# A hybrid decoder trunk on one core: rotary swap by DMA, main products in runs of 12 and 24, and a rearranged gate stage

## The chip, the core and the metric

One Trainium2 chip, of which this kernel uses one core. The core has TensorE (PE, with its weight loads shown apart as PEld), VectorE (DVE), ScalarE (ACT), GpSimd (POOL) and SyncE (SP), which here does nothing but start DMA transfers. The metric is the device time of one execution in microseconds.

## The reference, cut to what matters

One layer of a decoder: x goes through RMSNorm, one input projection, three attention head groups ("patterns") with windows and dilations (128, 1), (512, 4) and (2048, 16), a Mamba-2 branch (SSD) whose output is gated by silu(z) and normed, one output projection, and then a SwiGLU feed-forward. A prompt of 1024 positions and 8 decode positions with caches of 2048 rows are computed together. The parts that the change touches:

```python
def rope(x, pos):                       # q and k of all three patterns
    x1, x2 = xf[..., :half], xf[..., half:]          # half = 32
    return jnp.concatenate([x1 * cos - x2 * sin, x2 * cos + x1 * sin], axis=-1)
...
p = jnp.exp(sc - m); den = jnp.sum(p, axis=-1, keepdims=True)
o = jnp.einsum('brnhqk,brnkhd->brnhqd', p, vb) / den       # 128 keys and the 128 before them
...
def ssd_gate_out(y, xs, z, d_skip, ssd_norm_w):
    y = (y + d_skip[:, None] * xs).reshape(..., SSD_INNER) * jax.nn.silu(z)
    return rmsnorm(y, ssd_norm_w)
...
attn = merge_patterns(outs, lses)                          # softmax of the three lse, 512 columns
mix = jnp.concatenate([attn, ssm], axis=-1) @ w_out
```

## The kernel before

Everything lies transposed: features on the 128 partitions, the T = 1032 positions (1024 of the prompt, then 8 of decode) along the free axis, in three chunks CH of 344 columns. A matrix product in fp32 is made of three products on rounded parts: weight high times activation high, weight low times activation high, weight high times activation low. `unit` makes one 128 x 344 result from 8 blocks of 128 inputs, so 24 products, all on L175; `gemm` loads one 128 x 1024 weight (`load_w`: a DMA, then ACT rounds it to `wh` on L163 and DVE subtracts to `wl` on L164) and runs `unit` for the three chunks, each with a copy out of PSUM by ACT. PSUM has eight banks; the products of `unit` have the two of pool `psg` (tag g), the small work has the others: `pss` (tag sp, two banks) and the rest.

The order of instructions on each engine is fixed when the kernel is built, by a scheduler that takes, of the instructions whose inputs are ready in its own model of time, the one with the lowest priority number. `prio(kind)` hands out these numbers from counters: "evac" 1 million (copies out of PSUM and what follows at once), "w" 5 million (weight loads), "side" 10 million (attention, SSD and all small work), "late" 20 million (merging of the attention outputs and cache values), "main" 50 million (products of `unit`). So PE fills with main products whatever side work leaves, and a piece of side work may stand between any two main products. `behind(ins, prev)` fixes that an instruction stands behind another on its own engine. `next_copy` keeps the copies out of PSUM in order.

In time: up to some 200 us the projections of conv inputs; 200 to 590 us pattern 0 with the SSD work; to 890 us patterns 1 and 2; 850 to 968 us the gate stage; 968 to 1000 us the first products of the gated values with w_out (L955); to 1200 us output projection and norms; 1216 to 1592 us the feed-forward's inputs, then its outputs and the end.

In a pattern, each of four pairs of heads (hp) takes one `do_v` and two `do_qk` (q, then k), each of which is a projection of three units. The rotation in `do_qk` wants a copy `sw` of the projection `rw` in which each two neighbouring groups of 32 partitions have changed places: four ACT copies of 32 x 1032 on L615. POOL multiplies `sw` by sin on L616, DVE multiplies `rw` by cos on L617, and DVE adds both into `qr`. There are 24 rotations. `attend` then takes 8 steps per pair of heads, 96 in all: PE scores `sps` (L646), DVE adds the mask and takes the maximum (L652), ACT takes two exponentials with their sums (L660), PE transposes `ptp` (L667), a copy `pt` out of PSUM (ACT L671 in one step of four, DVE L673 in the other three), PE values `nps` (L680).

The gate stage: for each of 8 tiles k, the projection z (three units, copied to `zt` by ACT on L903), silu on ACT (L910), times the SSD result `yg`, loaded from DRAM `y_d`, on DVE (L911), the square on ACT (L916), and the sum of squares over the tiles, `acc`, by POOL (L918). `zt` has two buffers. In between stands "late" work: the merge (`nt` times weights on POOL L855, two adds on DVE L856 and L857, the rounding `ah` on ACT L858, `al` on DVE L859), 16 blocks of it; and the decode positions' values: for each b of 8, three cache blocks `cvt` times probabilities, added on DVE (L878), and summed over partitions by a product with `sel` (L879). After the tiles ACT and DVE split the gated values into `sh` (L924) and `sl` (L925), 128 x 1032 each; products with `ones` (L931 on `acc`, L932 on the last `zt`) sum the squares over partitions for the norm `rt`; and the first 96 products with w_out (L955) take two output tiles m and two chunks c at once.

Of the kernel before, what the change touches and what calls it, by code (L numbers as in the profile page):

```python
# [36 lines left out]
HB = T // 4  # L37
RATE = (0.35, 0.43)
# [11 lines left out]
def trunk(tc, a, o):  # L50
    nc = tc.nc
    ctr = {"evac": 1_000_000, "w": 5_000_000, "side": 10_000_000, "late": 20_000_000, "main": 50_000_000}
# [113 lines left out]

    def unit(ps, w, hs, ls, c, ch=CH):
# [14 lines left out]
    def gps(name="g", cw=CW):  # L182
# [4 lines left out]
        return q.tile([P, 512], F32, tag="ap", name=name)[:, :cw]  # L187

    def gemm(src, cols, hs, ls, evac, cc=(0, 1, 2), share=False):
# [440 lines left out]
    def attend(g, hp, qr, kr, vt):  # L630
        nh = nhp.tile([P, S], F32, tag="nh", name="nh")
        for j in range(8):
# [126 lines left out]
    with prio("side"):  # L759
        dec_scores(0)  # L760
    pattern(1)
# [49 lines left out]
    cvp = pool(rst, "cvp", 5, side="right")  # L811
# [49 lines left out]

    with prio("late"):
# [4 lines left out]
        for b in range(NB):  # L867
# [11 lines left out]
            nc.tensor.matmul(ops[:NB], sel[:, b * NB:(b + 1) * NB], vts[0], start=(b == 0), stop=(b == NB - 1))  # L879
# [12 lines left out]


    with prio("side"):
        rt = rowp.tile([P, T], F32, tag="row", name="rt")
        acc = gp.tile([P, T], F32, tag="acc", name="acc", bufs=1)
    yg = []
    for k in range(KT):
        zt = gp.tile([P, T], F32, tag="zt", name="zt")

        def ev(c, ps, zt=zt):
            c0, c1 = CH[c]
            return nc.scalar.copy(zt[:, c0:c1], ps)  # L903

        gemm(a["w_in"][36 + k], 1024, xh, xl, ev)
        with prio("side"):
# [587 lines left out]
```

## Time and profile before

| | us |
|---|---|
| median of 3 runs | 1859.24 |
| lowest and highest | 1858.23, 1863.11 |
| profiled execution, its own time | 1865.26 |
| span of that execution's profile | 1863.5 |
| PE busy in it | 1776.0 |
| DVE, ACT, POOL busy | 1141.2, 781.4, 320.0 |
| mean granted clock of TensorE | 0.98 of full speed |

The span reaches from the first to the last recorded instruction; 1.8 us of the execution lie around it. Busy times count an instruction from its start to its end, so matmuls that overlap in PE's pipeline count as one busy stretch, and a busy PE may still be slow. What PE loses is better seen in how many products it starts in a stretch.

### The profile page before, as it was taken

To read this page: it belongs to the slowest core of one execution; us is meant where nothing else is said; L and a number is where in the kernel's file an instruction comes from. 1 tells how busy PE (TensorE), PEld (TensorE's weight loads), DVE (VectorE), ACT (ScalarE), POOL (GpSimd) and SP (SyncE) were. 2 spreads that over 40 slices of the span, in tenths; PEclk is the share of its full clock that TensorE was granted. 3 is DMA by queue.
4 is the path that set the end of the run, shared out by engine and by line. 5 is a ranking of instruction groups with operands and counts; after the bars stand their busy time and mean duration, and the time that the engine had idled before them with its cause. 6 is when DMAs were issued, how large, how long until landed. Compare 5 with 4: busy or idle time off the path is not lost.

```text
span 1863.5 us, 30669 instructions
## 1 busy us (share of the span) xinstructions
PE 1776.0 (95%) x12183; PEld 1659.1 (89%) x12183; DVE 1141.2 (61%) x2228; ACT 781.4 (42%) x1433; POOL 320.0 (17%) x218
## 2 busy tenths in 40 slices
PE   8999999999998999999878999999999999999995
PEld 6999877888887889988758999999999999999995
DVE  6545666766765454446667499886666666423338
ACT  5533554455554555556333235532222222431133
POOL 0000245444234221123442301000000000000020
PEclk9999999999999999999988999999999999999998
DMA  4322344434334243346566355355545445976686
GB/s 157 135 100 79 97 127 125 128 121 116 114 103 156 90 137 103 123 152 224 171 167 182 101 160 180 110 199 171 176 151 183 167 151 197 351 264 215 207 314 206
DMA packets 135198, 298.59 MB, mean 160 GB/s; under 512 B 18432, under 2 KB 85600, under 8 KB 133648
## 3 DMA queue, kind: packets, MB, share of 16 engines
q1 hardware_dynamic: 135056, 296.64, 48.4%
q8 instruction: 95, 1.56, 0.3%
q14 instruction: 47, 0.39, 0.1%
HBM read 247.49 MB, written 137.10 MB: 206 GB/s over the span
## 4 chain that ended last, share of the span: by engine, by line
PE 37%; DVE 8%; DMA 3%; issue 1%; ACT 1%; POOL 1%; DVEq 0%; SPq 0%; POOLq 0%; ACTq 0%
PE fb L1217 20%; PE g L175 16%; DMA nt<-n_d 1%; PE g L955 1%; DVE xr L1043 1%; POOL nt L855 1%; DVE fl L1058 1%; DVE nacc L1000 1%; DVE mix L1055 0%; DVE nt L856 0%; DVE fac L1341 0%; DMA wr<-in_w_fin 0%; DVE nt L857 0%; DMA out_yT<-fac 0%; DMA wt<-w_d 0%
## 5 line engine op out<-in xcount | busy, mean ns | idle before, releaser
L175 PE MATMUL g<-xh,wh 128*128 128x344 f32 x1344 | 443.6, 330 | 9.3 <-ACT zt L903 5.1
L175 PE MATMUL g<-xl,wh 128*128 128x344 f32 x1344 | 440.3, 328 | 1.5 <-DVE xl L231 1.5
L175 PE MATMUL g<-xh,wl 128*128 128x344 f32 x1344 | 439.2, 327 | 0.5 <-DVE wl L164 0.5
L175 PEld LDWEIGHTS g<-xh,wh 128*128 128x128 f32 x1344 | 255.6, 190 | 19.0 <-ACT zt L903 5.6
L175 PEld LDWEIGHTS g<-xh,wl 128*128 128x128 f32 x1344 | 256.2, 191 | 12.3 <-issue 11.0
L175 PEld LDWEIGHTS g<-xl,wh 128*128 128x128 f32 x1344 | 256.1, 191 | 10.6 <-issue 7.7
L1217 PE MATMUL fb<-fh,wsl 128*128 128x258 f32 x1216 | 222.5, 283 | 0.1
L1217 PEld LDWEIGHTS fb<-fh,wsl 128*128 128x128 f32 x1216 | 188.0, 189 | 0.4 <-DVE fs L1113 0.3
L1217 PE MATMUL fb<-fl,wsl 128*128 128x258 f32 x608 | 171.9, 283 | 0.0
L164 DVE TENSOR_TENSOR wl<-wr,wh 128x1024 fp32r<-128x1024 f32 (+1 forms) x93 | 111.7, 1202 | 80.2 <-ACT wh L163 79.9
L175 PE MATMUL g<-hh,wh 128*128 128x344 f32 x432 | 138.1, 320 | 0.1
L175 PE MATMUL g<-hh,wl 128*128 128x344 f32 x432 | 137.8, 319 | 0.0
L175 PE MATMUL g<-hl,wh 128*128 128x344 f32 x432 | 136.9, 320 | 0.0
L163 ACT CAST wh<-wr 128x1024 fp32r<-128x1024 f32 (+1 forms) x93 | 92.5, 995 | 95.0 <-PE g L175 91.5
L660 ACT ACTIVATE sm<-sm,ngm 128x128 f32<-128x128 f32 (+1 forms) x192 | 84.9, 443 | 106.1 <-DVE ngm L656 102.2
L1300 POOL TENSOR_TENSOR ow<-wr,ow 128x512 fp32r<-128x512 f32 x8 | 10.9, 1395 | 658.8 <-ACT ow L1299 658.8
L616 POOL TENSOR_TENSOR sw<-sw,sin 128x1032 f32<-128x1032 f32 x24 | 72.8, 3032 | 251.0 <-ACT sw L615 187.6
L1217 PEld LDWEIGHTS fb<-fl,wsl 128*128 128x128 f32 x608 | 114.9, 189 | 0.0
L615 ACT COPY sw<-rw 32x1032 f32<-32x1032 f32 x96 | 101.0, 1052 | 1.4
L586 ACT COPY rw<-g 128x344 f32<-128x344 f32 x108 | 47.2, 443 | 111.8 <-PE g L175 71.5
L1221 DVE TENSOR_TENSOR fo<-fp,fb 128x258 f32<-128x258 f32 x152 | 62.8, 420 | 45.4 <-PE fb L1217 43.3
L175 PEld LDWEIGHTS g<-hh,wh 128*128 128x128 f32 x432 | 81.2, 188 | 0.3 <-ACT fac L1284 0.3
(362 smaller groups left out, 3801.2 us busy)
## 6 DMA issues: line engine op xcount, KB each, us to landing
out_skv<-in_cache SPq DMA_DIRECT2D x64, 1023.5 KB, 5.7
wr<-in_w_in SPq DMA_DIRECT2D x56, 512.0 KB, 3.7
out_skv<-in_cache SPq DMA_DIRECT2D x16, 1022.0 KB, 5.6
wr<-in_w_out SPq DMA_DIRECT2D x24, 512.0 KB, 3.7
hr<-hid_d SPq DMA_DIRECT2D x22, 516.0 KB, 6.2
hid_d<-fo SPq DMA_DIRECT2D x38, 258.0 KB, 4.5
wg<-in_w_fin SPq DMA_DIRECT2D x19, 512.0 KB, 4.2
wu<-in_w_fin SPq DMA_DIRECT2D x19, 512.0 KB, 5.1
```

Of the source, the lines that this page charges most:

```text
L163: nc.scalar.copy(wh[:, :cols], wr[:, :cols])
L164: nc.vector.tensor_tensor(out=wl[:, :cols], in0=wr[:, :cols], in1=wh[:, :cols], op=ALU.subtract)
L175: last = nc.tensor.matmul(ps, x[:, ws], y[:, c0:c1], start=(k == 0 and j == 0), stop=(k == n - 1 and j == 2))
L586: return nc.scalar.copy(rw[:, c0:c1], ps)
L615: nc.scalar.copy(sw[q * 32:(q + 1) * 32, 0:T], rw[s * 32:(s + 1) * 32, :])
L616: nc.gpsimd.tensor_tensor(out=sw[:, 0:T], in0=sw[:, 0:T], in1=sin, op=ALU.mult)
L660: nc.scalar.activation(out=sm[:, h, :nk], in_=sm[:, h, :nk], func=AF.Exp, scale=SCALE, bias=ngm[:, g, j, i:i + 1], accum_out=den[:, g, j, ...
L855: nc.gpsimd.tensor_tensor(out=nt, in0=nt, in1=wt, op=ALU.mult)
L955: nc.tensor.matmul(pq[m][c], ws[m][j == 1][:, k * P:(k + 1) * P], (sl if j == 2 else sh)[k][:, CH[c][0]:CH[c][1]], start=(k == 0 and j == ...
L1000: nc.vector.tensor_tensor(out=acc, in0=acc, in1=sq, op=ALU.add)
L1217: nc.tensor.matmul(ps, x[:, ks], y, start=(k == 0 and j == 0), stop=(k == 3 and j == 2))
L1221: return nc.vector.tensor_tensor(out=dst, in0=x, in1=y, op=ALU.add)
```

## The change

1. Runs. Of a unit's products, only each 12th carries the priority "main", the others a new priority "run" (3 million, ahead of weights and side work); from pattern 1 on, only each 24th. So side work on PE can stand only between runs of 12, later of 24, products.
2. Rotary swap. The four ACT copies of each rotation become four DMA transfers of 32 x 1032 fp32 (132 KB), started by SP. The product with sin moves from POOL to DVE.
3. All `pt` copies are on ACT: 72 more of them.
4. Gate stage. The loop over z stands ahead of the cache values in the code. From tile 4 on, the z units alternate over the two pools `psg` and `pss`, four banks. Each `sel` product stands behind the last product of a named z unit (table CACHE: tile, chunk). The cache values' pool has 6 buffers, not 5.
5. Sum of squares. POOL adds only the tiles up to 5; the products with `ones` take the squares of tiles 6 and 7 directly from their `zt` (nine products, not six), and stand behind the 48th of the 96 first products with w_out (`middle`).
6. The split into `sh` and `sl` is made in two column parts, 0 to 688 for all eight tiles, then 688 to 1032.

```diff
--- before
+++ after
@@ top of the file and trunk @@
+CACHE = ((4, 0), (4, 1), (4, 2), (5, 0), (5, 2), (6, 1), (7, 0), (7, 2))
...
-    ctr = {"evac": 1_000_000, "w": 5_000_000, "side": 10_000_000, "late": 20_000_000, "main": 50_000_000}
+    ctr = {"evac": 1_000_000, "run": 3_000_000, "w": 5_000_000, "side": 10_000_000, "late": 20_000_000, "main": 50_000_000}
@@ unit, gps, gemm @@
+    run = [12]
...
-        with prio("main"):
-            for k in range(n):
-                ws = slice(k * P, (k + 1) * P)
-                for j, (x, y) in enumerate(((wh, hs[k]), (wl, hs[k]), (wh, ls[k]))):
+        for k in range(n):
+            ws = slice(k * P, (k + 1) * P)
+            for j, (x, y) in enumerate(((wh, hs[k]), (wl, hs[k]), (wh, ls[k]))):
+                with prio("main" if (3 * k + j) % run[0] == 0 else "run"):
                     last = nc.tensor.matmul(ps, x[:, ws], y[:, c0:c1], start=(k == 0 and j == 0),
                                             stop=(k == n - 1 and j == 2))
...
-        return q.tile([P, 512], F32, tag="ap", name=name)[:, :cw]
+        return q.tile([P, 512], F32, tag="sp" if q is pss else "ap", name=name)[:, :cw]
...
+            if ends:
+                ends[0][ends[1], c] = last
@@ do_qk @@
-                nc.scalar.copy(sw[q * 32:(q + 1) * 32, 0:T], rw[s * 32:(s + 1) * 32, :])
-            nc.gpsimd.tensor_tensor(out=sw[:, 0:T], in0=sw[:, 0:T], in1=sin, op=ALU.mult)
+                nc.sync.dma_start(out=sw[q * 32:(q + 1) * 32, 0:T], in_=rw[s * 32:(s + 1) * 32, :])
+            nc.vector.tensor_tensor(out=sw[:, 0:T], in0=sw[:, 0:T], in1=sin, op=ALU.mult)
@@ attend @@
-            if j % 2 and j % 4 < 2:
-                nc.scalar.copy(dst, tp[:, :2 * nk])
-            else:
-                nc.vector.tensor_copy(dst, tp[:, :2 * nk])
+            nc.scalar.copy(dst, tp[:, :2 * nk])
@@ between dec_scores(0) and pattern(1) @@
+    run[0] = 24
@@ gate stage: the z loop now stands ahead of the cache values @@
-    cvp = pool(rst, "cvp", 5, side="right")
+    cvp = pool(rst, "cvp", 6, side="right")
...
+    zlast, zts = {}, []
     for k in range(KT):
+        if k == 4:
+            gpools[:] = [psg, pss]
         zt = gp.tile([P, T], F32, tag="zt", name="zt")
...
+        zts.append(zt)
+        gemm(a["w_in"][36 + k], 1024, xh, xl, ev, ends=(zlast, k))
...
-                if k < KT - 1:
+                if k < KT - 2:
                     nc.gpsimd.tensor_tensor(out=acc, in0=acc, in1=zt, op=ALU.add)
...
-            nc.tensor.matmul(ops[:NB], sel[:, b * NB:(b + 1) * NB], vts[0], start=(b == 0), stop=(b == NB - 1))
+            behind(nc.tensor.matmul(ops[:NB], sel[:, b * NB:(b + 1) * NB], vts[0], start=(b == 0), stop=(b == NB - 1)),
+                   zlast[CACHE[b]])
...
+    gpools[:] = [psg]
     sh, sl = [], []
     with prio("evac"):
         for k in range(KT):
-            hi = actp.tile([P, T], F32R, tag="act", name=f"sh{k}")
-            lo = actp.tile([P, T], F32R, tag="act", name=f"sl{k}")
-            nc.scalar.activation(out=hi, in_=yg[k], func=AF.Copy, scale=nw(SSD_NORM, k))
...
+            sh.append(actp.tile([P, T], F32R, tag="act", name=f"sh{k}"))
+            sl.append(actp.tile([P, T], F32R, tag="act", name=f"sl{k}"))
+        for cs_ in (slice(0, 2 * CW), slice(2 * CW, T)):
+            for k in range(KT):
+                hi, lo = sh[k][:, cs_], sl[k][:, cs_]
+                nc.scalar.activation(out=hi, in_=yg[k][:, cs_], func=AF.Copy, scale=nw(SSD_NORM, k))
+                nc.vector.scalar_tensor_tensor(out=lo, in0=yg[k][:, cs_], scalar=nw(SSD_NORM, k), in1=hi,
+                                               op0=ALU.mult, op1=ALU.subtract)
-        for c, (c0, c1) in enumerate(CH):
-            sp_ = att_ps("ptp")
-            nc.tensor.matmul(sp_[:, :CW], ones, acc[:, c0:c1], start=True, stop=False)
-            nc.tensor.matmul(sp_[:, :CW], ones, zt[:, c0:c1], start=False, stop=True)
-            rms(sp_[:, :CW], rt[:, c0:c1])
...
+                        if (k, m, j, c) == (3, 1, 2, 1):
+                            middle = ins
+    with prio("evac"):
+        for c, (c0, c1) in enumerate(CH):
+            sp_ = att_ps("ptp")
+            behind(nc.tensor.matmul(sp_[:, :CW], ones, acc[:, c0:c1], start=True, stop=False), middle)
+            for i in (KT - 2, KT - 1):
+                nc.tensor.matmul(sp_[:, :CW], ones, zts[i][:, c0:c1], start=False, stop=(i == KT - 1))
+            rms(sp_[:, :CW], rt[:, c0:c1])
```

SP, at a rotation of pattern 0 (`hs`, `out_sssm`, `in_ssm`: decode states of the SSD; `wr`: a weight), before:

```order
L469 DMA out_sssm<-hs_2000 128x4x128
L463 DMA hs_2018<-in_ssm 128x4x128
L469 DMA out_sssm<-hs_2009 128x4x128
L463 DMA hs_2027<-in_ssm 128x4x128
L469 DMA out_sssm<-hs_2018 128x4x128
L488 DMA xg_2036<-xs_d_326 128x4x128
L469 DMA out_sssm<-hs_2027 128x4x128
L148 DMA wr_4372<-in_w_in 128x1024
```

After, at the same place:

```order
L475 DMA out_sssm<-hs_2000 128x4x128
L621 DMA sw_3908<-rw_3823 32x1032 x3
L469 DMA hs_2018<-in_ssm 128x4x128
L149 DMA wr_4372<-in_w_in 128x1024
L621 DMA sw_3908<-rw_3823 32x1032
L475 DMA out_sssm<-hs_2009 128x4x128
L469 DMA hs_2027<-in_ssm 128x4x128
L475 DMA out_sssm<-hs_2018 128x4x128
```

The transfers of the swap stand in the one queue of SP; three are together, and the load of a state and of a weight come ahead of the fourth. In 14 of the 24 rotations the four are parted so.

PE, near the end of pattern 2 (`g`: a main unit; `nps`: values of the last attention step of a pair of heads; `vtp`: transposes of v for the next, by `do_v`), before:

```order
L175 MATMUL g_8809<-xl2_122,wh_8752 128x344
L175 MATMUL g_8809<-xh3_115,wh_8752 128x344
L175 MATMUL g_8809<-xh3_115,wl_8753 128x344
L175 MATMUL g_8809<-xl3_123,wh_8752 128x344
L680 MATMUL nps_7815<-pt_7859,vt_7523 64x128 x2
L604 MATMUL vtp_7956<-ident_90,vp_7954 128x128 x4
L175 MATMUL g_8809<-xh4_116,wh_8752 128x344
L175 MATMUL g_8809<-xh4_116,wl_8753 128x344
```

After, where the same `nps_7815` and `vtp_7956` stand:

```order
L652 MATMUL sps_8162<-qr_8157,qr_8061 128x128 x2
L683 MATMUL nps_7815<-pt_7827,vt_7523 64x128 x2
L652 MATMUL sps_8163<-qr_8157,qr_8061 128x128 x2
L673 MATMUL ptp_7843<-ident_90,sm_7837 128x128 x2
L683 MATMUL nps_7815<-pt_7846,vt_7523 64x128 x2
L673 MATMUL ptp_7856<-ident_90,sm_7850 128x128 x2
L652 MATMUL sps_8195<-qr_8157,qr_8061 128x128 x2
L652 MATMUL sps_8196<-qr_8157,qr_8061 128x128 x2
L683 MATMUL nps_7815<-pt_7859,vt_7523 64x128 x2
L610 MATMUL vtp_7956<-ident_90,vp_7954 128x128 x4
L791 MATMUL pnp_8387<-ident_90,pn0_8388 128x32
L791 MATMUL pnp_8387<-ident_90,pn1_8391 128x32
```

What stood between main products in pieces of two to six is now one piece with several attention steps and no main product in it. There are two such long pieces without main products: four steps near the 137th unit of PE, and eight steps near the 152nd. The piece begins where the first z tile's `zt` is to be used a second time: that wants its `yg` read, and the load of `yg` from `y_d` stands behind the last `vtp` of pattern 2 by the memory that it takes over. Before, that `vtp` stood five units ahead of this place.

PE, at the end of the z tiles (`g_9445` and `g_9330`: the last z unit; `ptp_9508`: sum of squares; `g_9547` to `g_9548` and `g_9543` to `g_9544`: first products with w_out), before:

```order
L175 MATMUL g_9445<-xh6_118,wh_9388 128x344
L175 MATMUL g_9445<-xh6_118,wl_9389 128x344
L175 MATMUL g_9445<-xl6_126,wh_9388 128x344
L175 MATMUL g_9445<-xh7_119,wh_9388 128x344
L931 MATMUL ptp_9508<-acc_8749,ones_91 128x344
L175 MATMUL g_9445<-xh7_119,wl_9389 128x344
L175 MATMUL g_9445<-xl7_127,wh_9388 128x344
L955 MATMUL g_9547<-sh0_9476,wh_9536 128x344
L955 MATMUL g_9548<-sh0_9476,wh_9536 128x344
L955 MATMUL g_9547<-sh0_9476,wl_9537 128x344
```

After:

```order
L179 MATMUL g_9330<-xh7_119,wl_9274 128x344
L179 MATMUL g_9330<-xl7_127,wh_9273 128x344
L913 MATMUL nps_9364<-cvt_9449,sel_9361 8x512
L958 MATMUL g_9543<-sh0_9475,wh_9532 128x344
L958 MATMUL g_9544<-sh0_9475,wh_9532 128x344
L958 MATMUL g_9543<-sh0_9475,wl_9533 128x344
L958 MATMUL g_9544<-sh0_9475,wl_9533 128x344
L958 MATMUL g_9543<-sl0_9476,wh_9532 128x344
```

The product with `acc` is gone from among the last z products, and stands after 48 products with w_out. The last `sel` product has come to the end of the last z unit. `sel` products stood before at the units 158.2 (three), 159.3, 160, 160.9, 163 and 164.2, counted in units of 24 main products; after, at 160 (two), 161 (three), 164, 166 and 168.

## Rows read from the trace of the kernel before

**Rows 1.** Part 1 of the page: busy us (share of the span) xinstructions.

```profile
PE 1776.0 (95%) x12183; PEld 1659.1 (89%) x12183; DVE 1141.2 (61%) x2228; ACT 781.4 (42%) x1433; POOL 320.0 (17%) x218
```

**Rows 2.** Stretches: length, busy us (xinstructions) of engines, granted clock, DMA share, GB/s.

```profile
50.00:100.00 50.00, 49.99 (x318) 49.99 (x319) 29.84 (x42) 24.19 (x32) 0.50 (x5) 1.00 0.34 117
...
900.00:950.00 50.00, 37.68 (x188) 28.60 (x186) 34.42 (x44) 13.01 (x22) 24.54 (x16) 0.94 0.69 188
950.00:1000.00 50.00, 41.54 (x206) 36.52 (x206) 37.22 (x45) 24.86 (x35) 19.18 (x9) 0.82 0.52 141
```

**Rows 3.** PE groups by line and form: xcount | busy us, mean ns | idle before.

```profile
L175 PE MATMUL g<-xh,wh 128*128 128x344 f32 x1344 | 443.6, 330 | 9.3 <-ACT zt L903 5.1 <-ACT rw L586 3.5 <-ACT wh L163 0.7
...
L646 PE MATMUL sps<-qr 64*128 64x128 f32 x208 | 25.8, 316 | 11.6 <-DVE qr L620 11.6
...
L497 PE MATMUL xt<-ident,xg 128*128 128x128 f32 x64 | 10.1, 280 | 7.7 <-DMA xg<-xs_d 7.7
...
L879 PE MATMUL nps<-cvt,sel 128*8 128x512 f32 x16 | 9.6, 705 | 7.6 <-DVE cvt L878 6.0 <-issue 1.6
...
L931 PE MATMUL ptp<-acc,ones 128*128 128x344 f32 x6 | 2.8, 562 | 3.0 <-POOL acc L918 3.0
```

**Rows 4.** ACT in order of time, at 947 us: start, us, instruction [idle before].

```profile
946.85 0.41 ACT L858 CAST ah<-nt 128x256 fp32r<-128x256 f32 x1 [6.25 <-DVE nt L857]
947.16 0.44 ACT L903 COPY zt<-g 128x344 f32<-128x344 f32 x1
```

**Rows 5.** PE in order of time, first products with w_out, 975 to 985 us.

```profile
975.60 0.94 PE L955 MATMUL g<-sh,wh 128*128 128x344 f32 x2 [2.19 <-ACT sh L924]
...
977.67 0.78 PE L955 MATMUL g<-sh,wh 128*128 128x344 f32 x2
...
982.16 0.94 PE L955 MATMUL g<-sl,wh 128*128 128x344 f32 x2 [1.43 <-DVE sl L925]
...
985.20 0.54 PE L955 MATMUL g<-sh,wh 128*128 128x344 f32 x2
```

**Rows 6.** Groups of the rotation and of the exponentials, by line and form.

```profile
L615 ACT COPY sw<-rw 32x1032 f32<-32x1032 f32 x96 | 101.0, 1052 | 1.4
...
L616 POOL TENSOR_TENSOR sw<-sw,sin 128x1032 f32<-128x1032 f32 x24 | 72.8, 3032 | 251.0 <-ACT sw L615 187.6 <-PE ptp L667 25.4 <-PE g L175 24.7
...
L617 DVE TENSOR_TENSOR rw<-rw,cos 128x1032 f32<-128x1032 f32 x24 | 38.6, 1610 | 18.6 <-ACT sw L615 18.6
...
L660 ACT ACTIVATE sm<-sm,ngm 128x128 f32<-128x128 f32 x104 | 41.0, 395 | 57.8 <-DVE ngm L656 54.3 <-PE nps L680 2.7 <-DVE stt L701 0.5
...
L660 ACT ACTIVATION_READ_ACCUMULATOR sm<-sm,ngm 128x1 f32 x192 | 36.0, 187 | 0.0
```

**Rows 7.** ACT and POOL in order of time, one rotation, 584 to 600 us.

```profile
584.52 4.24 ACT L615 COPY sw<-rw 32x1032 f32<-32x1032 f32 x4
...
596.79 2.36 POOL L616 TENSOR_TENSOR sw<-sw,sin 128x1032 f32<-128x1032 f32 x1
```

**Rows 8.** DMA issues (KB each, median us to landing), and SP's time for one.

```profile
yg<-y_d SPq DMA_DIRECT2D x8, 516.0 KB, 8.3
...
bg<-bc_d SPq DMA_DIRECT2D x16, 128.0 KB, 3.4
...
out_pv<-rw SPq DMA_DIRECT2D x4, 64.0 KB, 1.5
...
L627 SPq DMA_DIRECT2D out_pk<-qr x8: 338/344/352, 225.2 to 844.1; - x8
```

**Rows 9.** PE and ACT in order of time, one attention step, 765 to 767 us.

```profile
765.68 0.32 PE L175 MATMUL g<-xl,wh 128*128 128x344 f32 x1
765.93 0.44 PE L680 MATMUL nps<-pt,vt 128*64 128x128 f32 x4
...
766.49 0.41 PE L175 MATMUL g<-xh,wh 128*128 128x344 f32 x1
...
766.77 0.37 ACT L671 COPY pt<-ptp 128x256 f32<-128x256 f32 x1 [1.70 <-PE ptp L667]
```

More of the change, by code (lines that the diff above doesn't have):

```diff
@@ L859, in trunk, with ev @@
                 nc.vector.tensor_tensor(out=al[:, hp, qs], in0=nt[:, 0], in1=ah[:, hp, qs], op=ALU.subtract)
+    with prio("side"):
+        rt = rowp.tile([P, T], F32, tag="row", name="rt")
+        acc = gp.tile([P, T], F32, tag="acc", name="acc", bufs=1)
+    yg = []
+    zlast, zts = {}, []
+    for k in range(KT):
+        if k == 4:
+            gpools[:] = [psg, pss]
+        zt = gp.tile([P, T], F32, tag="zt", name="zt")
+        def ev(c, ps, zt=zt):
+            c0, c1 = CH[c]
+            return nc.scalar.copy(zt[:, c0:c1], ps)
+        zts.append(zt)
+        gemm(a["w_in"][36 + k], 1024, xh, xl, ev, ends=(zlast, k))
+        with prio("side"):
+            yt = mixp.tile([P, T], F32, tag="mix", name=f"yg{k}")
+            nc.sync.dma_start(out=yt, in_=y_d[k])
+        with prio("evac"):
+            nc.scalar.activation(out=zt, in_=zt, func=AF.Silu)
+            nc.vector.tensor_tensor(out=yt, in0=yt, in1=zt, op=ALU.mult)
+            yg.append(yt)
+            if k == 0:
+                nc.scalar.activation(out=acc, in_=yt, func=AF.Square)
+            else:
+                nc.scalar.activation(out=zt, in_=yt, func=AF.Square)
+                if k < KT - 2:
+                    nc.gpsimd.tensor_tensor(out=acc, in0=acc, in1=zt, op=ALU.add)
     with prio("late"):
@@ L891, in trunk @@
     rst.close()
[L894 to L906, printed above, removed]
-            yt = mixp.tile([P, T], F32, tag="mix", name=f"yg{k}")
-            nc.sync.dma_start(out=yt, in_=y_d[k])
-        with prio("evac"):
-            nc.scalar.activation(out=zt, in_=zt, func=AF.Silu)
-            nc.vector.tensor_tensor(out=yt, in0=yt, in1=zt, op=ALU.mult)
-            yg.append(yt)
-            if k == 0:
-                nc.scalar.activation(out=acc, in_=yt, func=AF.Square)
-            else:
-                nc.scalar.activation(out=zt, in_=yt, func=AF.Square)
-                if k < KT - 1:
-                    nc.gpsimd.tensor_tensor(out=acc, in0=acc, in1=zt, op=ALU.add)
+    gpools[:] = [psg]
     sh, sl = [], []
@@ L921, in trunk @@
         for k in range(KT):
[L922 to L934 removed]
+            sh.append(actp.tile([P, T], F32R, tag="act", name=f"sh{k}"))
+            sl.append(actp.tile([P, T], F32R, tag="act", name=f"sl{k}"))
+        for cs_ in (slice(0, 2 * CW), slice(2 * CW, T)):
+            for k in range(KT):
+                hi, lo = sh[k][:, cs_], sl[k][:, cs_]
+                nc.scalar.activation(out=hi, in_=yg[k][:, cs_], func=AF.Copy, scale=nw(SSD_NORM, k))
+                nc.vector.scalar_tensor_tensor(out=lo, in0=yg[k][:, cs_], scalar=nw(SSD_NORM, k), in1=hi,
+                                               op0=ALU.mult, op1=ALU.subtract)
     gpools.append(psa)
     ngp[0] = 0
[L939 removed]
     mix = [mixp.tile([P, T], F32, tag="mix", name=f"mix{m}") for m in range(KT)]
@@ L954, in trunk @@
                     for c in range(2):
-                        nc.tensor.matmul(pq[m][c], ws[m][j == 1][:, k * P:(k + 1) * P],
+                        ins = nc.tensor.matmul(pq[m][c], ws[m][j == 1][:, k * P:(k + 1) * P],
                                          (sl if j == 2 else sh)[k][:, CH[c][0]:CH[c][1]],
                                          start=(k == 0 and j == 0), stop=(k == KT - 1 and j == 2))
+                        if (k, m, j, c) == (3, 1, 2, 1):
+                            middle = ins
+    with prio("evac"):
+        for c, (c0, c1) in enumerate(CH):
[4 more added lines that the diff above has]
+            rms(sp_[:, :CW], rt[:, c0:c1])
+    gst.close()
+    np_ = pool(mst, "np", 2, side="left")
     with prio("evac"):
```

8 lines of the change are left out of this document (1 added, 7 removed).

## The prediction

> **What bounds the kernel now.** I read the busy shares first. PE is busy for 95% of the span and the next engine, DVE, for 61% [rows 1], so time is to be had only where PE starts fewer products than it could. The table of stretches shows where. At full clock with nothing in the way PE started 318 products in 50 us, 0.157 us each [rows 2]. In the gate stage, 900 to 1000 us, it started 188 + 206 = 394 matmuls of all kinds [rows 2]. At 0.157 these are 62 us. The 16 `sel` and 12 sum matmuls among them are longer; their spans of 0.705 and 0.562 us [rows 3] overlap, and I give them 7 us more. So 100 - 69 = 31 us are lost there, at a clock granted at 0.94 and 0.82 [rows 2]. Then I read the PE groups by the idle time before them, to see who is waited for: in the gate stage `zt` copies 5.1, `sel` 7.6, `acc` 3.0 us [rows 3], then `sh` 2.19 and `sl` 1.43 [rows 5]. Outside it, scores wait 11.6 us for `qr` and transposes 7.7 us for `xg` [rows 3]. Feed-forward and tail are untouched.
>
> **The gate stage, part by part.** *Sum of squares.* The products with `acc` stood among the last z products and made PE wait 3.0 us for POOL [rows 3]. They now stand behind 48 products of w_out, 7.5 us later at 0.157, and POOL has two adds less: **-3.0**. Three more products with `ones` come in, at most 0.562 us each [rows 3] and partly overlapped: **+1.0** (0.5 to 1.7).
>
> *Split in column parts.* PE waited 2.19 us for the first `sh` and 1.43 for an `sl` [rows 5]. Parts of 688 of 1032 columns are ready after two thirds of the time, and the third part follows while chunks 0 and 1 are multiplied. I take half: **-1.8** (0 to -3.6).
>
> *Clock.* From 975.60 to 985.20 us PE started 26 products of w_out [rows 5]. At 0.157 these are 4.1 us; they took 9.6, of which 1.43 were the wait for `sl`. The other 4.1 us is the slow clock after the waits ahead of them: the pace shown, 2.07 us for the six products from 975.60 to 977.67 [rows 5], is about half of full. With the waits ahead of it cut, PE should come there at full clock, except for some: **-3.3** (0 to -4.1).
>
> *Copies of z.* The group of first products waited 5.1 us for `zt` copies [rows 3]. ACT's timeline shows one cause: the copy at 947.16 stood behind a rounding `ah`, before which ACT had waited 6.25 us for the merge on DVE [rows 4]. ACT works in order, and that order is not changed. With four banks in place of two PE can run up to three units, 3 x 24 x 0.157 = 11 us, past a late copy, longer than the 6.25: **-4.6** (0 to -5.1). Against it stands that `zt` has only two buffers: a copy into a third tile still waits for the square of the first, so the banks help against a late copy and not against a late tile.
>
> *Cache values.* `sel` waited 7.6 us, 6.0 of it for DVE's adds [rows 3]. Pinned one to five units later (3.8 us each) with one buffer more, most should find their input ready. The last stands behind the last z unit and can still wait: **-5.6** (-2 to -7.6).
>
> Together -3.0 + 1.0 - 1.8 - 3.3 - 4.6 - 5.6 = **-17.3 us** of the 31 lost.
>
> **The rotary swap.** A rotation had four ACT copies of 1.05 us and a POOL product of 3.03 us on average [rows 6], and POOL was often not free: in the one at 584 us the copies ended at 588.8 and the POOL product began at 596.79 [rows 7], 8 us later. In its place come four transfers: SP needs 0.34 us for each issue [rows 8]. No row shows such a transfer of 132 KB. The nearest are 128 KB landing in 3.4 us and 64 KB in 1.5 [rows 8]; I take 2.4, between them. Then DVE's sin product, like its cos product 1.61 us [rows 6]. So 1.4 + 2.4 + 1.6 = 5.4 us (4.5 to 6.4) stand against 4.2 + 3.0 plus the queue on POOL, 7.2 to 15 us. Of the 11.6 us that scores waited for `qr` [rows 3] I take **-8** (-11.6 to 0). SP's queue is the risk, a rival below. DVE gains 24 x 1.61 = 39 us and loses 72 copies; ACT loses 101 us [rows 6] and gains 72 x 0.37 [rows 9] = 27. Both are further from PE's bound than before. The 7.7 us for `xg` [rows 3] is a wait of SSD work for loads in the same queue; with side work in larger pieces these have more time: **-3** (0 to -6, and +2 if the new transfers hold them up).
>
> **Runs of 12 and 24.** They change no product, only where side work may stand. Changes between main and side work on PE go from 216 to about 140. A change costs little: from the main product at 765.68 to the side product at 765.93 is 0.25 us, 0.09 over 0.157 [rows 9]. 76 of these are 7 us at most: **-2** (0 to -7). The cost is elsewhere. A pair's attention steps now come once in a unit or two, so attention falls behind, and at the end of pattern 2 there are 12 steps with no main product between them (four, then eight). A step alone goes at ACT's pace: two exponentials with their sums, 2 x (0.395 + 0.187) [rows 6], and a copy of 0.37 [rows 9], 1.53 us, where PE's own matmuls take about 1.1 (six of them took 765.93 to 766.49, 0.56 us [rows 9], and a step has some twelve). That is 12 x 0.45 = 5.4 us idle. After the eight, PE needs the `zt` that waits for the load of `yg`, 8.3 us [rows 8], and the product and copy behind it, about 1.8 us; against it some three steps' work, 4.6 us, and some decode work: about 5 us are left. Together **+10** (5 if the load comes early, 20 if nothing covers it and the clock falls in the gap).
>
> Patterns together: -8 - 3 - 2 + 10 = **-3**. In all -17.3 - 3 = -20.3. The profiled execution took 1865.26 us, 6 above the median; against it the sum gives 1845, and against the median of 1859.24, with which the new median will be compared, **1839 us**. A change of 0.3%, 5.6 us, is about what a measurement of this kernel can tell from none.
>
> A page of the Trainium skill speaks to the swap's price: "SBUF — State Buffer", section "Door 1: The DMA port swizzle (why `[64,N]` ≈ `[32,N]`)", says that DMA bandwidth goes by how many of 16 ports the partitions reach, and that 32 neighbouring partitions lie on half of them. By an estimate from that page's 435 GB/s, 132 KB would take 0.6 us in place of 0.3, later by 0.3 us for one. [...] No row here shows a transfer of this shape.
>
> **The rivals.** *A, all waits go.* The named waits of the gate stage go whole (3.0 + 3.6 + 4.1 + 5.1 + 7.6 - 1.0 = 22.4), the patterns give 11.6 + 6 + 2, and the bare stretches cost 5: -37, **1822**. For it: the clock falls only after waits, and one wait less saves the next. Against: the last cache value and the silu chain stay serial. Chance 0.17.
>
> *B, the bare stretches cost their upper end.* If the eight steps and the load of `yg` stand wholly bare, the runs cost 20 us, and the lower clock that follows a gap (0.82 in the last such stretch [rows 2]) takes some 4 more. -20.3 + 14 = -6, **1853 to 1858**, within 0.3% for the most part. For it: in the order no main product stands there. Against: the decode work in the same piece. Chance 0.13.
>
> *C, the transfers come late: slower.* The swap now goes through SP's single queue, where an instruction that waits holds all behind it. In 14 of 24 rotations the four transfers are parted by loads or stores that wait for other engines, and DVE's sin product, waiting, holds the masks of other steps and the `wl` of the next weight. PE then stands without scores and without weights. Each of the 24 rotations that costs 20/24 = 0.83 us more than forecast takes the gain away. At 1.5 us each it is +36 - 20 = +16: **1875**. For it: a load in this queue can take 8.3 us to land [rows 8], against the 2.4 taken. Against: main products cover most of a late `qr`, since each rotation has three units of 3.8 us beside it, and in 24 rotations before, with a chain of 7 to 15 us, PE waited only 11.6 us in all [rows 3]. Chance 0.18.
>
> *D, four banks that do nothing.* If tile buffers and not banks held the z units, the -4.6 goes and little else: 1844, inside the forecast.
>
> **How the numbers follow.** Forecast, with D, 1828 to 1850: 0.52. A 0.17, B 0.13, C 0.18. Faster by over 0.3% (below 1853.7): the forecast and A, 0.69. Within: most of B, 0.12. Slower: C and a tail of B, 0.19. For 8 in 10 the range takes in the forecast, most of A (all waits gone, and some of the clock with them: 1815) and B, and the milder half of C: 1815 to 1866.
>
> **What would show it.** In the stretches 900 to 1000 us of before, after: some 17 us less for the same products, and a clock near full from the z tiles into w_out. No wait for `acc` before the first products with w_out; `sel` waits below 2 us. The score's wait for `qr` below 4 us; swap transfers landing near 2.4 us, and DVE idle ahead of the sin product without PE idle beside it. Two idle stretches of PE at the end of pattern 2, 10 us together. Wrong would be: idle PE ahead of scores or ahead of main products for `wl`, transfers of over 5 us (C); over 20 us idle at the last steps (B); z products still waiting for `zt` (D).

## The result and the profile after

The changed kernel takes 1921.93 us (median of 4 runs, 1919.58 to 1924.64), where the kernel before took 1861.17 in the same session: 1.031 times as long, 95% interval 1.0282 to 1.0338. It was forecast at 1839 and 0.69 likely to be faster. The span of the profiled execution went from 1863.5 to 1917.8 us, by 54.3.

The busy shares after (part 1 of the page), to set beside [rows 1]:

```profile
PE 1797.8 (94%) x12189; PEld 1681.0 (88%) x12189; DVE 1109.9 (58%) x2188; ACT 711.5 (37%) x1419; POOL 243.0 (13%) x193
```

The other engines have less to do and PE has six matmuls more, as expected. So the 54 us are time in which PE waits or runs slowly. Added up over all matmuls of the trace, PE's idle time between its first and its last matmul grew from 68 to 101 us, by 33; the three products with `ones` that came in (six matmul records) add some 2; and the rest, some 19 us, is products that run slower: the mean granted clock fell from 0.980 to 0.962 of full speed.

Where: I compared the time at which PE had started the same number of main products, in units of 24. (These counts take in the 48 sum-of-squares matmuls at the start, so they run two units ahead of those under "The change".) Until unit 108 (some 627 us) the two kernels are level in main products; at unit 144 the changed one is 19 us late, at unit 156 38, at unit 174 48, at unit 210 58, and from unit 234 (the feed-forward) to the end constantly 54.5. But level in main products is not level in work. By 590 us both had started as many of them, and beside them the kernel before 1406 other matmuls, the changed one 1279. The missing 127 were put off, and come due at the end of attention.

The two long pieces without main products that the prediction named stand there, at 803.5 to 814.1 and at 882.7 to 911.9 us. In and just behind them PE is idle for 4.6 and 10.1 us. The stretches after, to set beside [rows 2]:

```profile
900.00:950.00 50.00, 43.64 (x256) 37.45 (x252) 24.79 (x54) 26.15 (x55) 19.26 (x13) 0.81 0.61 207
950.00:1000.00 50.00, 37.97 (x193) 31.38 (x194) 25.76 (x35) 12.95 (x21) 19.75 (x12) 0.84 0.55 133
1000.00:1050.00 50.00, 32.30 (x164) 27.87 (x162) 35.13 (x53) 25.13 (x41) 14.04 (x9) 0.83 0.45 136
```

Three such stretches in place of two, at a granted clock of 0.81 to 0.84. The PE groups that answer [rows 3] (the idle time before them is the last column):

```profile
L179 PE MATMUL g<-xh,wh 128*128 128x344 f32 x1344 | 450.6, 336 | 17.9 <-ACT rw L592 16.2 <-ACT zt L878 0.9 <-ACT wh L164 0.7
...
L652 PE MATMUL sps<-qr 64*128 64x128 f32 x208 | 27.0, 327 | 4.6 <-DVE mx L658 2.8 <-DVE qr L626 1.8
...
L503 PE MATMUL xt<-ident,xg 128*128 128x128 f32 x64 | 10.6, 290 | 4.4 <-DMA xg<-xs_d 4.4
...
L913 PE MATMUL nps<-cvt,sel 128*8 128x512 f32 x16 | 7.7, 593 | 0.0
...
L966 PE MATMUL ptp<-acc,ones 128*128 128x344 f32 x6 | 2.3, 470 | 1.2 <-ACT rt L205 1.2
```

Most waits that the prediction counted on did go: `zt` 5.1 to 0.9, `qr` 11.6 to 1.8, `sel` 7.6 to 0, `acc` 3.0 to 0. Those for `sh` and `sl` did not; they grew from 2.2 and 1.4 to 8.0 and 5.8. Others came in the place of those that went, first of all 16.2 us for `rw`, the copy of a projection (before: 3.5). PE's other large waits after (us in total, times, longest):

```profile
PE wtp L846 <- DVE wo L845: 14.2, 1, 14.2
PE g L958 <- ACT sh L936: 8.0, 1, 8.0
PE nps L683 <- ACT pt L676: 7.0, 12, 1.6
...
PE stp L757 <- DVE scs L753: 6.6, 2, 6.2
...
PE g L958 <- DVE sl L937: 5.8, 1, 5.8
```

**A wait for `rw` in the patterns.** PE, ACT and DVE of the changed kernel in order of time, at 634 us:

```profile
630.54 1.23 DVE L622 TENSOR_TENSOR sw<-sw,sin 128x1032 f32<-128x1032 f32 x1 [5.05 <-DMA sw<-rw]
...
634.68 2.41 DVE L626 TENSOR_TENSOR qr<-rw,sw 128x1024 f32<-128x1024 f32 x1
637.02 0.15 DVE L627 TENSOR_TENSOR dec<-rw,sw 128x8 f32<-128x8 f32 x1
...
637.25 0.79 ACT L592 COPY rw<-g 128x344 f32<-128x344 f32 x2 [3.90 <-DMA qb<-qd_d]
...
637.74 0.43 PE L179 MATMUL g<-xh,wh 128*128 128x344 f32 x1 [3.32 <-ACT rw L592]
```

`rw` has two buffers. The ACT copy at 637.25 starts when DVE's last reading of an older `rw` ends (637.02 + 0.15); before that instruction DVE waited for the swap's transfer. The PSUM bank is full until the copy, and PE has nothing else in its order. I read the copy's true releaser from these times; the row's own entry (`qb`) had long been done.

**The one long wait.** SP, PE and DVE at the end of attention:

```profile
939.85 6.82 SPq L905 DMA_DIRECT2D cvt<-in_cache  x2
...
945.81 0.44 PE L683 MATMUL nps<-pt,vt 128*64 128x128 f32 x4
...
951.00 0.33 SPq L905 DMA_DIRECT2D cvt<-in_cache  x1
...
951.50 2.08 SPq L823 DMA_DIRECT2D sn<-st_d  x3
...
960.02 0.55 DVE L845 TENSOR_TENSOR wo<-wg,md 128x64 f32<-128x64 f32 x3
...
960.40 0.39 PE L846 MATMUL wtp<-ident,wo 128*64 128x128 f32 x1 [14.15 <-DVE wo L845]
```

The last attention product ran at 945.81. In PE's order the transposes `wtp` of the merge weights come next. These need `wo`, which DVE and ACT work out from `sn` in small steps. SP issues the load of `sn` only at 951.50, behind a cache load for which it waited 3.3 us for a free buffer; load and steps then take until 960. PE has no main product in its order meanwhile and stands for 14 us.

**The swap's transfers** (DMA issues: KB, median us to landing):

```profile
sw<-rw SPq DMA_DIRECT2D x96, 129.0 KB, 2.4
```

They landed in a median of 2.4 us, the value taken (2.2 to 7.4). One issue cost SP 0.58 us (median), not the 0.34 of [rows 8].

### The profile page after: what moved, and what is told of

It reads as the page before. It is cut to its first block, busy times and chain, and to the rows that moved or that the text cites. A ratio compares the mean times of both kernels' runs of the same rounds, so it can differ in the third digit from the quotient of the medians.

```text
span 1917.8 us, 30783 instructions
## 1 busy us (share of the span) xinstructions
PE 1797.8 (94%) x12189; PEld 1681.0 (88%) x12189; DVE 1109.9 (58%) x2188; ACT 711.5 (37%) x1419; POOL 243.0 (13%) x193
## 5 line engine op out<-in xcount | busy, mean ns | idle before, releaser
L179 PE MATMUL g<-xh,wh 128*128 128x344 f32 x1344 | 450.6, 336 | 17.9 <-ACT rw L592 16.2
L179 PEld LDWEIGHTS g<-xh,wh 128*128 128x128 f32 x1344 | 259.7, 193 | 36.5 <-ACT rw L592 19.8
L179 PEld LDWEIGHTS g<-xh,wl 128*128 128x128 f32 x1344 | 260.3, 194 | 3.7 <-DVE wl L165 2.9
L658 DVE CUSTOM_DVE_ANT_0 sm<-sps,mask 128x128 f32<-128x128 f32 (+1 forms) x192 | 59.9, 346 | 81.6 <-PE ptp L673 48.3
L179 PEld LDWEIGHTS g<-hh,wl 128*128 128x128 f32 x432 | 81.2, 188 | 0.0
```

Of the source, the lines that this page charges most:

```text
L658: nc.vector.tensor_tensor_reduce(out=sm[:, h, :nk], in0=sps[h][:, c0:c0 + nk], in1=msk, scale=1.0, scalar=0.0, op0=ALU.add, op1=ALU.max, a ...
```

## Experiments: which part costs

**e1_runs_only, e2_swap_only, e3_gate_only** have one part of the diff each: parts 1; 2 and 3; 4 to 6. **e4_no_runs** is the changed kernel with part 1 undone:

```diff
-                with prio("main" if (3 * k + j) % run[0] == 0 else "run"):
+                with prio("main"):
```

> The kernel before with the runs of 12 and 24 main products alone. The changed kernel was 60 us slower. Theory R (runs: attention steps come later, so the merge and all behind it come later, and PE waits in pieces of steps): most of it here, 1895 to 1925 us. Theory S (rotary swap through SP's queue and copies on ACT): this alone 1850 to 1865. Theory G (rearranged gate stage): likewise 1850 to 1865.

> The kernel before with the rotary swap by transfers, the sin product on DVE and all pt copies on ACT. R: 1845 to 1860 (the waits for qr go). S: 1890 to 1920. G: 1845 to 1860.

> The kernel before with the rearranged gate stage alone (four banks, pinned sel products, two-part split, sums later). R: my forecast for this part alone, 1842, 1835 to 1855. S: the same. G: 1885 to 1920.

> The changed kernel with all main products at priority main again, so without runs. R: 1835 to 1850, faster than both. S and G: 1900 to 1925, hardly better than the changed kernel.

| kernel | median us | ratio to before | 95% interval |
|---|---|---|---|
| runs only | 1908.08 | 1.0235 | 1.021 to 1.026 |
| swap only | 1871.42 | 1.0038 | 1.0024 to 1.0053 |
| gate only | 1866.60 | 1.0014 | 0.9995 to 1.0032 |
| changed, no runs | 1864.69 | 1.0010 | 0.9997 to 1.0023 |

So the runs make the loss: alone they cost 44 us, and the changed kernel without them is 57 us faster than with them. But theory R was right in half only: the swap and the gate stage, each of which it expected to be faster than the kernel before, give nothing, alone or together. Both questions were followed.

For the swap PE's waits show the trade (swap only; us in total, times, longest):

```profile
PE g L175 <- ACT zt L900: 10.4, 2, 7.5
...
PE xt L497 <- DMA xg<-xs_d: 4.5, 3, 2.3
PE g L175 <- ACT rw L586: 4.0, 4, 1.5
PE sps L646 <- DVE qr L620: 4.0, 3, 1.5
PE sps L646 <- DVE mx L652: 3.9, 3, 2.3
PE nps L677 <- ACT pt L670: 3.7, 1, 3.7
```

`qr` fell from 11.6 to 4.0 and `xg` from 7.7 to 4.5, nearly the 11 us that were forecast for the two. `mx`, `pt` and, in the gate stage, `zt` took them back: PE's idle time is 70 us against 68. The swap and the `pt` copies on ACT were tried only together, so what each does is not shown.

## Experiments: why runs cost

In the kernel before with runs alone, `run` was varied: 6 everywhere (r6), 12 everywhere (r12), none in pattern 0 and 24 after (r24), and 24 from the gate stage on with none in the patterns (rz).

```diff
-    run = [12]
+    run = [6]     # r6; r12 keeps 12; r24 and rz: [1], so that every product is "main"
...
-    run[0] = 24   # ahead of pattern(1): left out in r6 and r12, kept in r24
...
+    run[0] = 24   # rz: ahead of the gate stage's pools
```

> The kernel before with runs of 6 in all stages. R, by the length of a run (12: +28 us): +8 to +18, 1871 to 1881. If what costs is the four and eight steps in one piece, which a run of 6 does not make: 1858 to 1867.

> The kernel before with runs of 12 in all stages, no 24. Theory R (a step's scores, transposes and values wait for the ends of runs, so attention lags with the run's length, and PE waits inside the pieces): 12 costs about half of the 44 us, 1875 to 1890. If only the few long pieces at the end of pattern 2 cost, which 24 makes: 1860 to 1870.

> The kernel before with runs of 24 from pattern 1 on and none in pattern 0. R: 1895 to 1908, nearly all of the 44 us, since until 700 us the runs of 12 had cost PE only 2 to 3 us. If pattern 0's lag is carried on: 1880 or less.

> The kernel before with runs of 24 only from the gate stage on, none in the patterns. Theory R (the cost of runs is attention's: its steps wait for run ends and PE waits in the pieces): 1858 to 1867, no change. If runs cost by holding the late work or the copies of z: 1870 to 1885.

From the traces: the start of the last value product of attention (`nps`), the units of main products that PE had started by then, and the last `al` of the merge.

| kernel | ratio (interval) | last nps, us | units | last al, us |
|---|---|---|---|---|
| before | 1 | 894.1 | 157.7 | 1035.9 |
| rz | 1.0015 (1.0002 to 1.0027) | 907.6 | 163.0 | 1043.8 |
| r6 | 1.0101 (1.0079 to 1.0122) | 919.1 | 160.5 | 1060.8 |
| r12 | 1.0154 (1.0135 to 1.0173) | 927.7 | 161.5 | 1066.5 |
| r24 | 1.0210 (1.0195 to 1.0226) | 929.2 | 160.0 | 1072.2 |
| 12, then 24 | 1.0235 (1.021 to 1.026) | 935.1 | 160.0 | 1077.6 |
| changed | 1.0310 (1.0282 to 1.0338) | 946.0 | 161.0 | 1090.2 |

Runs from the gate stage on cost next to nothing (rz), so the cost is attention's. (How rz comes to nothing follows below.) It rises with the length of a run and is already 19 us at six, where the longest piece from 590 us on holds two steps. So it is not only the few long pieces at the end, which was the size the prediction gave it. With 12 and 24, attention ends 41.0 us later. PE has 2.3 units more behind it then, worth 8.7 us, and the same 2026 other matmuls; the other 32 us PE has lost in the patterns. Added up from the traces, 21 of them are idle time (58.5 us up to the last `nps`, 37.4 before), and the rest is slower products (mean granted clock up to there 0.962, before 0.987). Of the 21, 12 came before 590 us, in pattern 0, and 8 behind 850 us, around the last long piece. PE's largest waits over the whole span (runs only, then one of the kernel before):

```profile
PE g L178 <- ACT rw L589: 23.3, 10, 7.2
PE g L178 <- DVE wl L164: 9.4, 4, 5.8
PE sps L649 <- DVE mx L655: 8.6, 4, 4.8
...
PE g L175 <- DVE wl L164: 3.7, 3, 1.9
```

Before, they were 3.5, 3.7 and none. Of the 23.3 us for `rw`, 18.5 lie in pattern 0; the `mx` waits lie in the patterns too, the longest in the last long piece. Of the 9.4 for `wl`, 8.9 come behind attention, from 1034 us on, and belong to the stage after it. An explanation that fits is that a step which may enter PE only between runs frees its buffers later, and the next products wait for them. No row here follows such a wait back to the end of a run, so this link is argued, not shown. With no runs of 12 in pattern 0 (r24) it is 1902.82 us, against 1908.08; the intervals of the two ratios overlap, so these add some 5 us, if anything.

## Experiments: why the gate stage gives nothing

**q1** leaves 12 of the 16 merge blocks out, in four kernels: before, gate only, runs only, and the changed one.

```diff
                 qs = slice(q * QT, (q + 1) * QT)
+                if q:
+                    nc.scalar.copy(ah[:, hp, qs], ah[:, hp, 0:QT])
+                    nc.vector.tensor_copy(al[:, hp, qs], al[:, hp, 0:QT])
+                    continue
```

> The kernel before, with 12 of the 16 merge blocks left out (their ah and al are copied from the first quarter: no load, no POOL product, no adds). In five runs so far the first product on ah starts 154 to 158 us behind the last nps of attention, whatever the rest does. Theory M: that serial chain of merge blocks (6.9 us each) sets the end of the mixer, and PE's waits in the gate stage lie in its shadow. Then leaving out 12 blocks takes time off until PE's own work is the bound: 1825 to 1845. Rival P: PE is the bound, the chain runs beside it: 1855 to 1863.

> The kernel before with the rearranged gate stage, and with the same 12 merge blocks left out. M: out of the chain's shadow the gate stage gives what was forecast, 8 to 17 us less than the same cut without it. P: within 4 us of it.

> The kernel before with runs of 12 and 24, and with the same 12 merge blocks left out. With all blocks the runs cost 44 us. M: the part of it that is only the later start of the chain goes, and the part that PE loses waiting inside the pieces stays: 15 to 28 us over the same cut without runs. P: all 44 stay.

> The changed kernel with the same 12 merge blocks left out. M: 10 to 25 us over the kernel before with the same cut (pieces' waits, less the gate's gain). P: 55 to 60 over it.

| kernel | median us | ratio to before (whole) | 95% interval |
|---|---|---|---|
| q1_before | 1845.61 | 0.9909 | 0.9885 to 0.9933 |
| q1_gate | 1845.62 | 0.9907 | 0.9893 to 0.9922 |
| q1_runs | 1879.79 | 1.0091 | 1.0076 to 1.0106 |
| q1_after | 1906.33 | 1.0228 | 1.0202 to 1.0254 |

The blocks cost 18 us in the kernel before; the forecast, which had given them no term, did not see it. That is about the number of theory M, but not its way. M has the end of the chain hold the first product on `ah`. In q1_before that product starts at 1027.9 us, and PE is 23 us ahead of the kernel before already at 1013; its idle time from 900 to 1050 us is 12 us in place of 24. The stretch from 950 on, to set beside [rows 2]:

```profile
950.00:1000.00 50.00, 48.82 (x299) 46.73 (x298) 31.28 (x35) 24.95 (x33) 2.41 (x1) 1.00 0.25 82
```

It has 299 matmuls in place of 206, at a clock of 1.00 in place of 0.82. So in the kernel before the blocks cost by what they do to PE within the gate stage. Nor is the distance from the last `nps` to the first product on `ah` fixed at 154 to 158 us, as M took it: it is 140 us in r12 and 138 in rz.

Without the 12 blocks the gate stage still gives nothing, as rival P had it. One reason is in the waits of q1_before: those for `acc`, `sh` and `sl` are gone with the blocks, and of what the gate stage was to win back only `zt` (5.8) and `sel` (4.5) are left. Of the 44 us of the runs 34 stay, and the changed kernel is 61 over the same cut; for these M was wrong. So the blocks account for 10 us of the cost of the runs alone.

What the gate stage does is to rename waits. PE's waits with the gate stage alone:

```profile
PE g L176 <- DVE wl L165: 10.4, 6, 3.7
...
PE g L957 <- DVE sl L936: 5.5, 1, 5.5
...
PE g L957 <- ACT sh L935: 3.0, 1, 3.0
...
PE nps L912 <- DVE cvt L911: 2.0, 1, 2.0
```

Before, these four with `zt` and `acc` were 23.0 us (3.7, 1.4, 2.2, 7.6 with 1.6 of issue, 5.1, 3.0). Now they are 20.9. The wait for `sl` shows why, in order of time:

```profile
970.21 3.57 POOL L858 TENSOR_TENSOR nt<-nt,wt 128x768 f32<-128x768 f32 x2 [6.48 <-DMA nt<-n_d]
...
972.05 2.01 DVE L859 TENSOR_TENSOR nt<-nt 128x256 f32<-128x256 f32 x1 [4.34 <-POOL nt L858]
973.98 1.41 DVE L936 SCALAR_TENSOR_TENSOR sl<-yg,par,sh 128x688 fp32r<-128x688 f32 x2
...
974.96 0.94 PE L957 MATMUL g<-sl,wh 128*128 128x344 f32 x2 [5.46 <-DVE sl L936]
```

POOL waits for a merge block's load, DVE stands behind POOL with the block's add, the split stands behind it on DVE, and PE behind the split. Here a smaller split does not help, since it stands behind a load.

**n3** gives the block's data `nt` three buffers (the kernel before, and the changed one without runs and with five buffers for cache values); **pm** puts the block's adds, rounding and `al` on POOL (the same two); **pn** does both (before, and gate only).

```diff
-                nt = mgp.tile([P, NG, QT], F32, tag="nt", name="nt")
+                nt = mgp.tile([P, NG, QT], F32, tag="nt", name="nt", bufs=3)      # n3, pn
...
-                nc.vector.tensor_tensor(out=nt[:, 0], in0=nt[:, 0], in1=nt[:, 1], op=ALU.add)
-                nc.vector.tensor_tensor(out=nt[:, 0], in0=nt[:, 0], in1=nt[:, 2], op=ALU.add)
-                nc.scalar.copy(ah[:, hp, qs], nt[:, 0])
-                nc.vector.tensor_tensor(out=al[:, hp, qs], in0=nt[:, 0], in1=ah[:, hp, qs], op=ALU.subtract)
+                nc.gpsimd.tensor_tensor(out=nt[:, 0], in0=nt[:, 0], in1=nt[:, 1], op=ALU.add)   # pm, pn
+                nc.gpsimd.tensor_tensor(out=nt[:, 0], in0=nt[:, 0], in1=nt[:, 2], op=ALU.add)
+                nc.gpsimd.tensor_scalar(out=ah[:, hp, qs], in0=nt[:, 0], scalar1=1.0, scalar2=0.0, op0=ALU.mult,
+                                        op1=ALU.add)
+                nc.gpsimd.tensor_tensor(out=al[:, hp, qs], in0=nt[:, 0], in1=ah[:, hp, qs], op=ALU.subtract)
```

> The kernel before with three buffers in place of two for the merge's nt (the weights keep two). In the runs so far a block's load waits until al of the block two earlier has left its buffer, 6.9 us a block, and DVE and ACT stand in order behind it. Theory M (this chain is the bound from the last attention step to the first product on ah): pace 5 us or less and 10 to 20 us faster, 1843 to 1853. If loads or in-order queues set the pace and not the buffers: within 4 us of before.

> The changed kernel without runs (swap and gate stage kept), with three nt buffers and five for cache values. M: what is left of the gate's gain comes on top of the faster chain, 1835 to 1852. Otherwise 1860 to 1868, as without the third buffer.

> The kernel before with each merge block's two adds, rounding and al on POOL, behind its own product there, in place of DVE and ACT. Theory Q: DVE and ACT work in order and stand at a merge block whose load has not come, with weights (wl), z copies and splits behind them; so PE's waits in the gate stage only change names when the gate is rearranged. Then this frees them: 1845 to 1857. If the bound is the chain of blocks itself or DVE's work, nothing or slower: 1860 to 1872, since POOL is slower at the same adds.

> The changed kernel without runs, with the merge blocks wholly on POOL. Q: the gate's rearrangement now gives what it was forecast to, on top of the last: 1832 to 1850. Otherwise as without it, 1860 to 1870.

> The kernel before with the merge blocks wholly on POOL and with three nt buffers. With POOL alone PE was 13.8 us ahead at the 180th unit and then lost 14.4 in one wait for wah, the weight for the products on ah, whose memory the last merge block gives up; with the third buffer alone the chain ended 21 us earlier and PE was not ahead. Theory B (two bounds that hide each other: PE held in order by the blocks, and the chain of blocks): both together 1845 to 1858. If the third buffer only brings blocks forward in the order, again: 1862 to 1872.

> The same two edits and the rearranged gate stage (five buffers for cache values), without runs and without the swap. B: with both bounds eased the gate's own gain shows, 3 to 12 us under pn_before. If the gate stage gives nothing by itself: within 4 us of pn_before.

| kernel | ratio | 95% interval | last al, us | first product on ah, us |
|---|---|---|---|---|
| before | 1 | | 1035.9 | 1051.1 |
| n3_before | 1.0038 | 1.0023 to 1.0053 | 1014.4 | 1054.7 |
| n3_noruns | 1.0043 | 1.0022 to 1.0063 | 1021.4 | 1054.8 |
| pm_before | 1.0015 | 1.0002 to 1.0028 | 1049.8 | 1051.7 |
| pm_noruns | 1.0044 | 1.0027 to 1.0060 | 1059.4 | 1061.3 |
| pn_before | 1.0031 | 1.0013 to 1.0049 | 1038.9 | 1053.6 |
| pn_gate | 1.0028 | 1.0018 to 1.0039 | 1036.4 | 1051.8 |

None is faster, and theories M, Q and B each missed as the gain that they promised. They still tell something. With n3 the blocks end 21 us earlier and PE is no earlier: they now stand further forward in the engines' order, and PE waits there (`sel` 8.8, `acc` 8.3 us). With pm PE is 13.8 us ahead at unit 180 and loses it in one wait:

```profile
PE g L175 <- ACT wah L981: 14.4, 1, 14.4
```

`wah`, the weight for the products on `ah`, is rounded into memory that the last block gives up, and on POOL the blocks end at 1050. With both edits POOL's blocks were no faster than in the kernel before (last `al` 1038.9), so pn did not shorten the chain as theory B wanted and is no test of it. It shows the same tie (ACT, in order of time):

```profile
1039.67 1.04 ACT L981 CAST wah<-wr 128x1024 fp32r<-128x1024 f32 x1 [13.87 <-POOL al L860]
1040.62 1.04 ACT L163 CAST wh<-wr 128x1024 fp32r<-128x1024 f32 x1
```

ACT stands 13.87 us at `wah` until the last `al`, and behind it the weight `wh` of an earlier output tile, for which PE waits 6.9 us.

rz, with runs from the gate stage on and the blocks as they were, came to the same place. At unit 184 PE is 21 us ahead of the kernel before, with the same 2061 other matmuls done: its idle time up to there is 49 us in place of 61, and the granted clock from 850 us on 0.96 in place of 0.92. So PE does win with runs, in the gate stage, what the rearrangement was to win. But the last `al` comes at 1043.8 us, and PE gives back most of its lead in one wait:

```profile
PE g L178 <- ACT wah L984: 16.0, 1, 16.0
```

In the kernel before PE does not wait there (ACT and PE, in order of time):

```profile
1038.81 1.05 ACT L980 CAST wah<-wr 128x1024 fp32r<-128x1024 f32 x1 [2.90 <-DMA wr<-in_w_out]
...
1051.05 0.32 PE L175 MATMUL g<-ah,wah 128*128 128x344 f32 x1
```

`wah` is ready 11 us before PE comes to its first product on `ah`. So two things bound this part. In the kernel before it is PE behind engines that stand at blocks. The end of the blocks has 11 us to spare there, and takes what PE wins beyond that; more, where an edit delays the blocks as well, as pm and rz do. By these rows I estimate that of the 17.3 us forecast for the gate stage not more than some 11 could have shown. What eased one bound lost on the other; rz with a shorter chain of blocks was not tried.

## Why the prediction was wrong, by its own steps

**The bound.** The prediction took 95% busy PE and 31 us lost in the gate stage as PE's own to win back. The chain of waits of the page was not used for that stage, and it names the blocks there (loads of `nt`, POOL and DVE on `nt`, `al`) from 919 us to 1019. Its end in the kernel before (start us, us, what):

```profile
1005.40 8.10 DMA nt<-n_d
1013.66 1.86 POOL nt L855
1015.55 0.44 DVE nt L856
1016.35 0.51 DVE mix L239
1016.86 2.35 DVE wl L164
1019.26 24.29 PE g L175 x143
```

A block's load, its product on POOL and its add on DVE stand ahead of a weight `wl` in DVE's order, and PE goes on when that weight is there. This is the first step that failed: that cutting a named wait of PE shortens the stage. q1_before shows 18 us hanging on the blocks, for which the prediction had no term.

**Gate stage, -17.3.** Measured alone: +0.14%, -0.05 to +0.32, so nothing. The single steps came as described (`acc`, `sel` and `zt` waits gone after), but -1.8 for `sh` and `sl` was 3.6 turned into 8.5 (gate alone) and 13.8 (after), and `wl` rose by 6.7. Its condition "parts are ready after two thirds of the time" left out what stands ahead of the parts on DVE. The slow clock, -3.3, followed the waits and stayed: from 950 to 1000 us 0.86 was granted with the gate stage alone, 0.82 before. Why the gate stage gives nothing even without 12 blocks is settled only in part: against q1_before, PE is 6 us ahead at unit 168 and 2 behind at 174. The sums and the last `sel` were moved into that unit range, so it holds 168 matmuls in place of 152, with 1.8 us of waits where there were none. The edits of the stage were not tried one by one.

**Rotary swap, -8, and xg, -3.** The size of the chain was right (2.4 us to land), the issue at 0.58 us was dearer, and the two waits fell by 10.8. But the whole part cost 0.38%. The step that failed was again that a wait that goes is time gained. Rival C's mechanism, late transfers, did not decide by itself: the swap alone is 7 us over the kernel before, so 15 over its forecast of -8, and not 36. Rival C had the direction of the whole right, with 0.18, but for the most part by luck: 44 of the 58 us are the runs alone. By the page "SBUF — State Buffer" of the Trainium skill (section "Door 1: The DMA port swizzle (why `[64,N]` ≈ `[32,N]`)"), transfers of 32 partitions reach half of the ports; what that costs here no run shows. These transfers between two places on the chip landed in 2.4 us and the 128 KB loads from DRAM of [rows 8] in 3.4, but the two differ in more than the partitions.

**Runs, +10 and -2.** These +8 were mis-sized by more than five: +44, which alone turns the forecast gain into a loss. Rival B had the term at 24 at most. The pieces of steps without main products came as described, and their idle time was near its size: 14.7 us in the two pieces of the changed kernel, of which the wait for `zt` was 0.9 in place of 5. What failed is that only these 12 bare steps were counted. The traces show work put off and waits for `rw` already in pattern 0, and slower products after them; with runs alone 32 us are lost before the last attention product and some 12 behind it; 10 of these 44 us go with 12 blocks left out.

**Changed kernel as a sum.** The prediction added its parts. 1.0235 x 1.0038 x 1.0014 = 1.029 is near the 1.031 measured, but swap and gate stage together give 1.0010, and 1.0235 x 1.0010 = 1.0245 lies below its interval (1.0282 to 1.0338). So beside the runs these two cost some 12 us that they do not cost without them, and 27 us with 12 blocks left out (1879.79 to 1906.33). PE's idle time ahead of `wtp` is of that kind: 14.2 us in the changed kernel, 5.6 with runs alone, 4.1 in the changed kernel without runs. No run has the runs with only one of the two, so which of them adds it stays open. No version tried beats the kernel before with all of its work done.

## What to carry to other kernels

A wait of the busiest engine is worth its length only if nothing else ends just behind it: before counting idle time as gain, follow the chain of waits through that stage and ask which load or chain the engines in front stand at. Side work that feeds a busy engine needs many short openings; here runs of six main products already cost 1%. When two orders are compared by how far the main work has come, count the side work too: what was put off comes due later. A rearrangement that moves waits from one name to another should be priced by the sum of all waits of the stage, not by the names that vanish.

## What was not expected of the hardware

- SP needed 0.58 us (0.51 to 1.60) to issue one transfer of 32 x 1032 between two places on the chip, where the store of [rows 8] took 0.34.
- Waits came with more than their length: beside 33 us more idle time the mean granted clock fell from 0.980 to 0.962, and some 19 us more went on slower products.
